# A hybrid attention and delta-rule step on one core: later products for transposed probabilities, and branch B's product with w_b during the second half's attention

## Chip, core and metric

The kernel runs on one core of a Trainium2 chip. The metric is the device time of one execution in microseconds, lower is better. Engines are named as in the profile: PE (TensorE, with PEld for its weight loads), DVE (VectorE), ACT (ScalarE), POOL (GpSimd) and SP (SyncE), which in this kernel issues every DMA.

## What is computed

One layer over 2048 prompt frames and 32 sampled frames of width 1024. The reference, cut to what the change touches:

```
qa, ka, va, za, qkv_b, zb, a_b, b_b, gate_a, gate_b = split_projection(x @ w_in)
oa = chunk_band_attention(qa, ka, va, rel_bias)      # 8 heads of 64, 9 chunks of 64 keys
ya = (oa * silu(za)) @ w_branch_a
ob, s_new = gated_delta_rule(...)                     # branch B, then a norm per head
yb = (ob * silu(zb)) @ w_branch_b
mix = sigmoid(gate_a) * ya + sigmoid(gate_b) * yb
y = layer_norm(ALPHA * x + mix @ w_out)
```

The newest 512 rows of k and v, and those of the sampled frames, are outputs too.

## The kernel before

The frames are worked off in two halves of 1024 (the second with the 32 sampled frames). For each half a stream of projection jobs (`all_jobs`, L2022; `multiply`) runs on TensorE: 128 columns of w_in times all frames of the half, split into a high and a low f16 part, so three products per 128 rows. Beside these jobs runs first branch B (`phase_b`), then attention (`phase_a`, L1492). After the second half's attention comes the merge (L2157): for each of 8 blocks of 256 frames the gated outputs of both branches are multiplied by w_a and w_b, weighted by the gates, added, multiplied by w_out and normalised.

**What sets the order.** The kernel is written as many small streams (Python generators) which a planner, the class `Flow`, runs while the program is built. It keeps a clock per engine, adds an estimated price for every instruction and DMA, and lets the stream go on that is earliest by these clocks. The result is a fixed order of instructions on each engine and of DMAs on SP's queue. On the chip every engine takes its instructions in that order and waits at each until its inputs are there. A price in the planner thus changes no work, only the order. `transfer` (L211) returns the time at which a DMA is thought to have landed; `turn` (L301) does so for a DMA transpose; `gate` and `places` are counted slots, `mark` an event.

**Attention.** Per pair of heads p, jobs v, k, q and z bring the operands. k and q are split into f16 high and low parts. `kst` holds for each head its high part in its own 64 partitions and the low part in the other 64; `qd` holds the high part of q in both; so one product over 128 rows gives high times high plus high times low. A second product, with the low part of q, completes the score (`score`, L1804). For it `ql` (`low_q`, L1523) is a tile of [128, 2, 1024] with zeros in the other head's partitions. The scores get their bias and maximum on VectorE, the exponential on ScalarE, and are split again into f16 parts `pu`. A DMA transpose turns `pu` into `pt`, with which TensorE makes the product with v into bank "c" (`product`). `store` (L1892) loads the gate `ga` (from za), transposes the normalised output in a "b" bank and writes the result to `g_dram[0]`. There are two "b" banks, three "a", two "pj" and one "c". Rows of k and v go out by `rows_out` (L1554): for each 128 rows a transpose into a "b" bank, a copy to one of two `ro` tiles and a DMA.

**Fetching.** `fetch` (L619) loads the weights of all jobs in order through two raw tiles, and after the last job w_a and w_b. `claim_w` (L771) gives them their room: w_a in a pool of its own, w_b in the room of the normalised input, which is free only after the last projection.

**Merge.** `load_g` (L2135) brings the branch outputs of a block and splits them, `sg_ahead` (L2253) the gates (three tiles per branch), and `merge` runs, for each of 8 column groups f and both branches, 12 products of 256 columns: four with the high and low part of the weights and the high part of g, then four with the low part of g. VectorE multiplies the sum by the gate (`evac`) and adds the branches (`fold`). For block 0 the order of (f, branch) starts with three groups of w_a (`order`, L2151).

Of the kernel before, what the change touches and what calls it, by code (L numbers as in the profile page):

```python
# [21 lines left out]
P = 128  # L22
# [37 lines left out]
MARGIN = 1.6  # L60
LEAD = 5.0
# [44 lines left out]
class Places(Gate):  # L106


    def __init__(self, flow, n):
        super().__init__(flow, n)  # L110
        self.numbers, self.first = deque(range(n)), False

    def ask(self, s):
        super().ask(s)
        if self.first and self.queue and self.queue[-1] is s:
            self.queue.rotate(1)
        self.first = False

    def take(self, first=False):
        self.first = first  # L120
        yield self
        return self.numbers.popleft()
# [97 lines left out]

def width(ap):
    n = 1
    for k in ap.shape[1:]:
        n *= k
    return n
# [52 lines left out]
def trunk(ctx: ExitStack, tc: tile.TileContext, x_p, x_s, cache_k, cache_v, st_conv, st_gdn,  # L278
# [22 lines left out]
    def turn(dst, src):  # L301

        nc.sync.dma_start_transpose(dst, src)
        n = 2 * P
        for k in dst.shape[1:]:
            n *= k
        return flow.transfer("SP", n * 1.5)
# [311 lines left out]
    def fetch(jobs):  # L619

        for job in jobs:
            yield raw_gate
            raw = wpool.tile([P, KD, P], F32, tag="wraw", bufs=NRAW, name="wraw")
            if job.cols < P:
                G.memset(raw[:], 0.0)
                yield
            for c0, part in job.src:
                for k0 in range(0, KD, 4):
                    t = dma(raw[:, k0:k0 + 4, c0:c0 + part.shape[2]], part[:, k0:k0 + 4, :])
            q_raw.put((job, raw, t))  # L630
            yield

        jobs_near.done()
        for br, w in enumerate((w_a, w_b)):
            yield from claim_w(br)
            for k in range(NP):
                yield raw_gate
                wr = wpool.tile([P, KD, P], F32, tag="wraw", bufs=NRAW, name="wr")
                wr = wr[:].rearrange("p k n -> p (k n)")
                t = dma(wr, w[k * P:(k + 1) * P, :])  # L640
                both = [None, raw_gate.give]
                for c in range(2):
                    flow.start(split_w(br, k, c, wr[:, c * 512:(c + 1) * 512], t, both[c]))
                yield
        for _ in range(NRAW):
            yield raw_gate
        front_w.done()

# [158 lines left out]
    def job_gate(half, br, f):  # L807
        def evac(bi, c0, n, gcol, ps):
            yield sig_slots
            t = wpool.tile([P, 512], F32, tag="sig", bufs=2, name="sig")  # L810
            S.activation(out=t[:, 0:n], in_=ps[:, 0:n], func=AF.Tanh, scale=w_half[:, wid:wid + 1])
            bank["pj"].give()
            yield
            yield dma(sig_dram[br][f][:, gcol:gcol + n], t[:, 0:n])
            sig_slots.give()

        wid = 32 + 8 * br + f
        return Job(half, wid, [(0, w_in[wid])], evac)

    rest = [[job_gate(half, br, f) for br in range(2) for f in range(KD)] for half in range(2)]  # L820


# [669 lines left out]
    def phase_a(half):  # L1492
# [8 lines left out]
        ro_slots, bias_slots, vs_slot, sample_slot = gate(2), [gate(2), gate(1)], gate(2), gate(1)  # L1501
# [21 lines left out]
        low_q = []  # L1523
        for i in range(2):
            t = ap.tile([P, 2, HALF], F16, name=f"ql{i}")
            for h in range(2):
                G.memset(t[HS[1 - h], h], 0.0)
            low_q.append(t)
# [25 lines left out]
        def rows_out(src, n, dst, p):  # L1554

            for t in range(0, n, P):
                m = min(P, n - t)
                yield bank["b"]
                ps = pt("b")
                PE.transpose(ps[:m, 0:P], src[:, t:t + m], ident[:])  # L1560
                yield ro_slots
                ro = ap.tile([P, P], F32, tag="ro", bufs=2, name="ro")
                S.copy(out=ro[:m], in_=ps[:m, 0:P])
                bank["b"].give()
                yield
                yield dma(dst[t:t + m, p * P:(p + 1) * P], ro[:m])
                ro_slots.give()

        def job_v(k):
# [9 lines left out]
            def rest():  # L1579
# [32 lines left out]
                if last:  # L1612
# [9 lines left out]
                    yield from rows_out(vf[:, KW:KW + DEC], DEC, nv_s, p)  # L1622
# [62 lines left out]
        def job_q(k):  # L1685
# [3 lines left out]
            def begin():  # L1689
# [11 lines left out]
                k.ql = ql = low_q[p % 2]  # L1701
# [102 lines left out]
        def score(h, k, t, w, place, before, turn_):  # L1804
# [8 lines left out]
            for i, (s0, sn) in enumerate(pieces):  # L1813
# [5 lines left out]
                PE.matmul(ps[:, 0:sn], ql[:, h, t * P:(t + 1) * P], kst[:, h, kc + s0:kc + s0 + sn],  # L1819
# [72 lines left out]
        def store(k, t, gt, w):  # L1892
# [7 lines left out]
            at = dma(ga[:], za_dram[k.p][:, gt * P:(gt + 1) * P])  # L1900
# [220 lines left out]
    g_slot, m_slot, x_slots = gate(1), gate(1), gate(3)  # L2121
    SGB = 3
    sg_slots = [gate(SGB), gate(SGB)]
    q_g, q_x, q_sg = [Queue(flow), Queue(flow)], [Queue(flow), Queue(flow)], Queue(flow)
# [9 lines left out]

    def load_g():  # L2135
        yield jobs_near
        for b in range(NB):
            c0 = b * FB
            n = FB if b < NB - 1 else FW
            yield g_slot  # L2140
            for br in range(2):
                ghi = gp.tile([P, NP, FW], F32R, tag=f"ghi{br}", bufs=1, name="ghi")
                glo = gp.tile([P, NP, FW], F32R, tag=f"glo{br}", bufs=1, name="glo")
                m = [[mark() for _ in range(NP)] for _ in range(2)]
                t = dma(glo[:, :, 0:n].bitcast(F32), g_dram[br][:, :, c0:c0 + n].rearrange("q p t -> p q t"))
                for p in range(NP):
                    flow.start(split_g(ghi, glo, p, m, n, t))
                q_g[br].put((ghi, glo, m))
                yield

    def order(b):  # L2151
        todo = [(f, br) for f in range(KD) for br in range(2)]
        if b == 0:
            todo.sort(key=lambda w: w[0] if w[0] >= SGB else w[1] - 2)
        return todo

    def merge():  # L2157
        yield jobs_done
        for b in range(NB):
            c0, n = b * FB, FB if b < NB - 1 else FW  # L2160
            gs = [None, None]
# [28 lines left out]

            all_parts, all_both = [[] for _ in range(KD)], [[0] for _ in range(KD)]
            for f, br in order(b):
                parts, both = all_parts[f], all_both[f]
                sg, t = yield from q_sg.get()
                parts.append(sg)
                yield bank["a"]
                ps = pt("a")
                if f == 0:
                    gs[br] = yield from q_g[br].get()
                gh, gl, ready = gs[br]  # L2200
                for k in range(NP):
                    yield w_ready[br, k, f // 4]
                    wh, wl = (w[f // 4][:, :, f % 4 * P:(f % 4 + 1) * P] for w in wres[br])
                    yield ready[0][k]
                    PE.matmul(ps[:, 0:n], wh[:, k], gh[:, k, 0:n], start=(k == 0), stop=False)
                    PE.matmul(ps[:, 0:n], wl[:, k], gh[:, k, 0:n], start=False, stop=False)
                    yield
                for k in range(NP):
                    yield ready[1][k]
                    PE.matmul(ps[:, 0:n], wh[:, k], gl[:, k, 0:n], start=False, stop=(k == NP - 1))  # L2210
                    yield

                def evac(f=f, sg=sg, ps=ps, t=t, parts=parts, both=both):
                    yield t
                    V.scalar_tensor_tensor(out=sg[:, 0:n], in0=sg[:, 0:n], scalar=1.0, in1=ps[:, 0:n],
                                           op0=ALU.add, op1=ALU.mult)
                    bank["a"].give()
                    yield
                    both[0] += 1
                    if both[0] == 2:  # L2220
                        yield from fold(f, parts)

                flow.start(evac())
            g_slot.give()

# [27 lines left out]
    def sg_ahead():  # L2253
        yield jobs_near
        for b in range(NB):
            n = FB if b < NB - 1 else FW
            for f, br in order(b):
                yield sg_slots[br]
                sg = gp.tile([P, FW], F32, tag=f"sg{br}", bufs=SGB, name="sg")
                t = dma(sg[:, 0:n], sig_dram[br][f][:, b * FB:b * FB + n])  # L2260
                q_sg.put((sg, t))
                if b == 0:
                    yield t - LEAD

# [80 lines left out]
    for half in range(2):  # L2345
# [5 lines left out]
        if half:  # L2351
# [3 lines left out]
            for gen in (load_g(), sg_ahead(), merge()):  # L2355
# [68 lines left out]
```

## Time and profile before

| | |
|---|---|
| time before, median of 3 runs | 2080.12 us (2076.62 to 2083.29) |
| the profiled execution: its time | 2078.09 us |
| its span, first to last instruction | 2076.3 us |
| mean granted TensorE clock | 0.973 |
| DMA transposes pt<-pu | 128 |
| loads of gates in the merge, sg<-sig | 128 |

A row of the windows gives the stretch, its length, the busy time of each engine with the number of instructions, the granted clock, the mean share of the 16 DMA engines and the data rate. A row of a tile gives the operation, the tile written and those read, the count, the minimum, median and maximum duration in ns, first and last start, and the shapes; 64*32 is 64 rows and 32 columns of the array. A row of the waits gives who waited for what, the total, how often, and the longest. A row in order of time gives start, duration, and in brackets the idle time before it and what ended it. Nearly every instruction bears the line of the helper that records it (L269; DMAs L292 and L303), so tiles tell them apart.

### The profile page before, as it was taken

The numbers are of one execution on the slowest core, as the hardware profiler recorded it, in microseconds if no ns is written. First come the engines' busy times: TensorE is split into PE (matmuls) and PEld (weight loads), VectorE is DVE, ScalarE is ACT, GpSimd is POOL, SyncE is SP. The second block draws the span as 40 slices with busy tenths as digits, with TensorE's granted clock in tenths as the row PEclk, the third lists the DMA queues.
The fourth block names the chain that finished last, engine by engine and source line by source line (L and its number), as shares of the span: only waits on it lengthen the run. The fifth ranks groups of instructions, "written<-read, shape, count | busy, mean of one in ns | idle before, by whom it ended". The sixth has DMA issues, their size and how long they took to land. (4 is left out here: it accounts for less than half of the span.)

```text
span 2076.3 us, 41078 instructions
## 1 busy us (share of the span) xinstructions
PE 1930.5 (93%) x14517; PEld 1353.4 (65%) x14517; DVE 1400.7 (67%) x4498; ACT 972.5 (47%) x2002; POOL 796.0 (38%) x1139
## 2 busy tenths in 40 slices
PE   8999999999989899999999999998888879999997
PEld 5455666665444446576776777665555568999996
DVE  7789889852556658589889884254545468665665
ACT  6655545444655667665445434354646552111110
POOL 6444334333334334443333423132323245543452
PEclk9999999999999999999999999999999989999999
DMA  4124332332587775223232333466776785433331
GB/s 138 65 87 112 87 85 75 102 90 98 140 201 158 163 171 135 69 81 87 74 84 67 94 98 90 117 142 146 158 167 148 186 217 193 132 102 122 103 124 46
DMA packets 380055, 246.85 MB, mean 119 GB/s; under 512 B 251202, under 2 KB 328366, under 8 KB 379848
## 3 DMA queue, kind: packets, MB, share of 16 engines
q1 hardware_dynamic: 379848, 244.22, 44.4%
q8 instruction: 114, 1.87, 0.4%
q14 instruction: 93, 0.76, 0.1%
HBM read 140.11 MB, written 54.72 MB: 94 GB/s over the span
## 5 line engine op out<-in xcount | busy, mean ns | idle before, releaser
L269 PE MATMUL pj<-hi,whi 128*128 128x512 f16 (+2 forms) x1992 | 651.3, 342 | 10.6 <-DVE zb L269 3.1
L269 PE MATMUL pj<-hi,wlo 128*128 128x512 f16 (+2 forms) x1952 | 643.6, 342 | 0.6 <-POOL wlo L269 0.5
L269 PEld LDWEIGHTS <-whi 128*128 128x128 f16 x3984 | 414.7, 106 | 226.0 <-issue 11.9
L269 PE MATMUL pj<-lo,whi 128*128 128x512 f16 (+2 forms) x1992 | 460.3, 343 | 0.0
L269 POOL TENSOR_TENSOR wlo<-wraw,whi 128x256 f16<-128x256 f32 x384 | 266.7, 718 | 497.4 <-ACT whi L269 369.5
L269 PEld LDWEIGHTS <-wlo 128*128 128x128 f16 x1952 | 207.1, 106 | 122.8 <-issue 16.6
L269 ACT CAST mh<-sg 128x256 fp32r<-128x256 f32 x64 | 25.8, 407 | 278.2 <-DVE sg L269 259.1
L269 ACT ACTIVATE wraw<-wraw,w_scale 128x1024 f32<-128x1024 f32 (+1 forms) x98 | 111.4, 1136 | 84.2 <-DVE w_scale L269 82.7
L269 ACT ACTIVATE sb<-sb,mx,unit 128x640 f32<-128x640 f32 (+4 forms) x128 | 108.5, 848 | 68.9 <-DVE mx L269 59.1
L269 PE MATMUL a<-ghi,whi 128*128 128x256 f32 (+1 forms) x512 | 134.4, 292 | 6.7 <-DVE sg L269 6.1
L269 POOL TENSOR_TENSOR pu<-sb,pu 128x640 f16<-128x640 f32 (+2 forms) x64 | 81.7, 1277 | 146.1 <-ACT pu L269 92.9
L269 ACT CAST whi<-wraw 128x512 f16<-128x512 f32 (+1 forms) x196 | 119.2, 611 | 33.3 <-PE pj L269 30.5
L269 PE MATMUL c<-vt,pt 128*128 128x64 f16 x1680 | 74.6, 198 | 64.5 <-DMA pt<-pu 61.4
L269 PE MATMUL a<-ghi,wlo 128*128 128x256 f32 (+1 forms) x512 | 132.0, 288 | 1.1 <-POOL wlo L269 1.0
L269 PEld LDWEIGHTS <-pt 128*128 128x128 f16 x1680 | 65.8, 101 | 98.8 <-DMA pt<-pu 87.1
L269 DVE TENSOR_TENSOR sys_u<-sys_u,sys_t 128x60 f32<-128x60 f32 (+24 forms) x527 | 124.6, 242 | 5.7
L269 DVE CUSTOM_DVE_ANT_0 sb<-a,bias 128x320 f32<-128x320 f32 (+5 forms) x136 | 66.5, 498 | 77.0 <-PE a L269 71.5
L269 DVE SCALAR_TENSOR_TENSOR acc<-raw,cwT,acc 128x512 f32<-128x512 f32 x144 | 112.8, 783 | 8.1 <-ACT acc L269 6.8
L269 DVE TENSOR_TENSOR sys_t<-sys_u,sys_p 128x60 f32<-128x60 f32 (+21 forms) x459 | 110.0, 243 | 5.5
L269 PEld LDWEIGHTS a<-ghi,whi 128*128 128x128 f32 x512 | 99.5, 194 | 8.3 <-DVE sg L269 6.7
L269 PEld LDWEIGHTS a<-ghi,wlo 128*128 128x128 f32 x512 | 98.9, 193 | 1.9 <-POOL wlo L269 1.2
L269 POOL TENSOR_TENSOR w_scale<-w_scale,mhalf 128x1 f32<-128x1 f32 x49 | 31.7, 648 | 168.1 <-DVE w_scale L269 120.0
(345 smaller groups left out, 4013.5 us busy)
## 6 DMA issues: line engine op xcount, KB each, us to landing
wraw<-in_w_in SPq DMA_DIRECT2D x192, 256.0 KB
sg<-sig SPq DMA_DIRECT2D x112, 128.0 KB
sig<-sig SPq DMA_DIRECT2D x44, 256.0 KB
sys_p<-sol_p SPq DMA_DIRECT2D x68, 128.0 KB
x<-in_x_p SPq DMA_DIRECT2D x16, 512.0 KB
xt<-in_x_p SPq DMA_DIRECT2D x16, 512.0 KB
out_y_p<-xt SPq DMA_DIRECT2D x16, 512.0 KB
glo<-g SPq DMA_DIRECT2D x14, 512.0 KB
```

Of the source, the lines that this page charges most:

```text
L269: r = f(*a, **k)
```

## The change

Four things are changed.

1. In the planner a transpose takes 0.8 us more of SP's queue and is thought to land SLACK = 2.5 us later; the load of `ga` gets the same 2.5 us.
2. `ql` is a tile of [128, 1024] without zeros. The second score product takes the 64 partitions of its head, of `ql` and of `kst`. One DMA per block of q fills it instead of two, and the zeros are no longer set.
3. `rows_out` transposes up to four groups of rows into one bank and writes them with one copy and one DMA (a remainder of less than 128 rows with another); there is one `ro` tile. The v rows of the sampled frames are written from `v_s`.
4. w_b is fetched before job z of pair 0 of the second half, into the pool that w_a had; w_a comes at the end, into the room of the normalised input. A new stream `early` starts when w_b is split. For block after block that the merge hasn't claimed it loads g of branch B, and for each f the gate; when the planner's TensorE has less than 0.2 us of work ahead, it makes the 12 products in a "b" bank, multiplies by the gate and writes the weighted result over the gate in DRAM. The merge leaves out branch B for such blocks and loads the finished values in the gate's place. Blocks 4 to 7 also wait for the second half's gates of branch B, whose jobs now come ahead of branch A's. `early` ends once w_out is ready.

```
-        return flow.transfer("SP", n * 1.5)
+        flow.busy["SP"] = max(flow.busy.get("SP", 0.0), flow.cur.clock + 0.2) + 0.8
+        return flow.transfer("SP", n * 1.5) + SLACK
...
+            if job.half == 1 and job.key == EARLY:
+                yield from load_w(1, w_b)
...
-        if br:
+        if br == 0:
             for g in h_free:
                 yield g
         else:
             yield wr_open
-        pool = hpool if br else wr_pool[0]
+        pool = wr_pool[0] if br else hpool
...
+    rest = [[job_gate(half, br, f) for br in ((0, 1) if half == 0 else (1, 0)) for f in range(KD)] for half in range(2)]
...
-                    t = dma(ql[HS[h], h, cs], lo[HS[h], 0:m])
+                t = dma(ql[:, cs], lo[:, 0:m])
...
-                PE.matmul(ps[:, 0:sn], ql[:, h, t * P:(t + 1) * P], kst[:, h, kc + s0:kc + s0 + sn],
+                PE.matmul(ps[:, 0:sn], ql[HS[h], t * P:(t + 1) * P], kst[HS[h], h, kc + s0:kc + s0 + sn],
                           start=False, stop=True)
...
-            at = dma(ga[:], za_dram[k.p][:, gt * P:(gt + 1) * P])
+            at = dma(ga[:], za_dram[k.p][:, gt * P:(gt + 1) * P]) + SLACK
```

The new rows_out and the new stream:

```
+            yield bank["b"]
+            ps = pt("b")
             for t in range(0, n, P):
                 m = min(P, n - t)
+                PE.transpose(ps[:m, t:t + P], src[:, t:t + m], ident[:])
+            yield ro_slots
+            ro = ap.tile([P, 512], F32, tag="ro", bufs=1, name="ro")
+            if full:
+                S.copy(out=ro[:, 0:full * P], in_=ps[:, 0:full * P])
...
+                at = dma(dst[0:full * P, cs].rearrange("(t q) d -> q t d", q=P),
+                         ro[:, 0:full * P].rearrange("q (t d) -> q t d", d=P))
...
+    def early():
+        for k in range(NP):
+            for c in range(2):
+                yield w_ready[1, k, c]
+        for b in range(NB):
+            c0, n = b * FB, FB if b < NB - 1 else FW
+            if b in claimed_b or w_ready["o", KD - 1, 1].at is not None:
+                return
+            claimed_b[b] = "early"
+            yield g_early
+            g = get_g(1, b)
+            for f in range(KD):
+                if b == NB // 2:
+                    yield gate_done[1, 1, f]
+                yield sge_slots
+                sg = gp.tile([P, FW], F32, tag="sge", bufs=2, name="sge")
+                t = dma(sg[:, 0:n], sig_dram[1][f][:, c0:c0 + n])
+                while w_ready["o", KD - 1, 1].at is None and flow.busy["PE"] > flow.cur.clock + 0.2:
+                    yield flow.busy["PE"]
+                yield bank["b"]
+                ps = pt("b")
+                yield from branch(1, f, n, ps, g, t - MARGIN)
...
+                    V.scalar_tensor_tensor(out=sg[:, 0:n], in0=sg[:, 0:n], scalar=1.0, in1=ps[:, 0:n],
+                                           op0=ALU.add, op1=ALU.mult)
+                    bank["b"].give()
+                    yield
+                    yield dma(sig_dram[1][f][:, c0:c0 + n], sg[:, 0:n])
+                    sge_slots.give()
...
+            g_early.give()
```

More of the change, by code (lines that the diff above doesn't have):

```diff
@@ L110, in __init__, with take @@
         super().__init__(flow, n)
[L111 to L120, printed above, removed]
+        self.numbers = deque(range(n))
+    def take(self):
         yield self
@@ L633, in fetch @@
         jobs_near.done()
[L634 to L644, printed above, removed]
+        yield from load_w(0, w_a)
         for _ in range(NRAW):
@@ L2151, in order, with claim_block @@
[L2151 to L2155, printed above, removed]
+            gs = [get_g(0, b)]
+            if not claim_block(b):
+                yield g_early
+                gs.append(get_g(1, b))
+            q_g.put(gs)
+            yield
+    def claim_block(b):
+        if b not in claimed_b:
+            claimed_b[b] = "merge"
+        return claimed_b[b] == "early"
@@ L2189, in fold @@
                 m_ready[1][f].done()
[L2191 to L2195, printed above, removed]
+            g = None
+            for f in range(KD):
+                parts = []
+                for br in range(2):
+                    parts.append((yield from q_sg.get()))
                 yield bank["a"]
@@ L2208, in merge @@
[L2208 to L2213, printed above, removed]
-                    yield t
[L2215 to L2221, printed above, removed]
```

153 lines of the change are left out of this document (100 added, 53 removed).

## Prediction

> **What bounds the kernel now.** I read the page first, then five stretches of the span, then TensorE's waits in the two attention stretches, then single moments of them in order of time.
>
> ```profile
> span 2076.3 us, 41078 instructions
> PE 1930.5 (93%) x14517; PEld 1353.4 (65%) x14517; DVE 1400.7 (67%) x4498; ACT 972.5 (47%) x2002; POOL 796.0 (38%) x1139
> ```
>
> TensorE (PE) is busy for 93% of the span, so the kernel is bound by TensorE's work and by the holes in it. The windows say where the holes are; the columns are busy time per engine, the granted TensorE clock, the DMA share and GB/s.
>
> ```profile
> core 0: us, PE busy (x) PEld busy (x) DVE busy (x) ACT busy (x) POOL busy (x), PEclk, DMA share, GB/s
> 500.00:820.00 320.00, 286.98 (x2089) 158.00 (x2087) 189.19 (x687) 197.88 (x389) 120.18 (x153) 0.97 0.68 162
> 820.00:1290.00 470.00, 454.91 (x3840) 333.96 (x3840) 382.09 (x1318) 233.94 (x501) 178.51 (x317) 0.98 0.29 80
> 1290.00:1662.00 372.00, 323.63 (x2712) 210.72 (x2711) 172.01 (x598) 196.54 (x407) 100.32 (x111) 0.95 0.66 153
> 1662.00:1700.00 38.00, 29.74 (x298) 24.71 (x297) 25.49 (x85) 19.05 (x39) 11.35 (x9) 0.82 0.75 176
> 1700.00:2076.00 376.00, 359.33 (x2247) 323.81 (x2245) 240.66 (x424) 55.68 (x143) 171.94 (x208) 0.99 0.39 125
> ```
>
> The first row is the first half's attention: 320 - 287.0 = 33.0 us without TensorE work. The third and fourth are the second half's attention, first beside the projections, then alone: 48.4 + 8.3 = 56.7 us. The last is the merge; it is nearly full (16.7 us idle), and DMA is little used there. The stage to look at is therefore attention. Who ends TensorE's waits there (total us, times, longest), first half and then second:
>
> ```profile
> PE c L269 <- DMA pt<-pu: 25.5, 19, 3.3
> ```
>
> ```profile
> PE c L269 <- DMA pt<-pu: 35.9, 23, 3.8
> PE b L269 <- DVE ga L269: 6.2, 6, 2.3
> PE b L269 <- ACT za L269: 2.8, 1, 2.8
> ```
>
> Two thirds of the idle time, 61.4 us, is the product of the probabilities with v waiting for their transposes (pt<-pu, by DMA). TensorE takes its instructions in an order fixed at build time, and the build thought the transposes would land earlier than they do. Such a wait costs more than itself:
>
> ```profile
> 1439.68 0.28 PE L269 MATMUL pj<-hi,whi 128*128 128x272 f16 x1
> 1439.80 0.28 PE L269 MATMUL pj<-hi,wlo 128*128 128x272 f16 x1
> 1442.53 0.61 PE L269 MATMUL c<-vt,pt 128*128 128x64 f16 x15 [2.46 <-DMA pt<-pu]
> ...
> 1443.70 0.43 PE L269 MATMUL pj<-hi,whi 128*128 128x272 f16 x1
> 1443.93 0.43 PE L269 MATMUL pj<-hi,wlo 128*128 128x272 f16 x1
> ```
>
> Before the wait of 2.46 us the same product started every 0.12 us, about a microsecond after it every 0.23 us: the clock is at half. The windows give the price: TensorE's busy time times the missing clock is 287.0 x 0.03 = 8.6, 323.6 x 0.05 = 16.2 and 29.7 x 0.18 = 5.4 us, 30 us in all. So the waits on transposes stand for up to 61.4 + 30 = 91 us. [...]
>
> **Room for the transposes.** The planner (which only decides the order) now charges each transpose 0.8 us more on SyncE's queue and lets it land another 2.5 us later, so 3.3 us of other work is put ahead of each product with v. That is as long as the longest wait of the first half (3.3 us) and nearly that of the second (3.8), so on an unchanged pipeline almost all 91 us would go. What is late next is SyncE, which issues every DMA, transposes among them:
>
> ```profile
> 1450.02 0.44 SPq L292 DMA_DIRECT2D g<-ga  x1
> ...
> 1498.47 1.89 SPq L292 DMA_DIRECT2D kst<-part  x3
> ```
>
> ```profile
> L303 SPq DMA_TRANSPOSE pt<-pu x128: 1167/1356/2562, 550.7 to 1691.0; - x128
> ```
>
> Between these first and last rows lie 51 issues that take 41.8 of 50 us, a transpose alone 1.36 us. With SyncE at 84%, part of the lateness is a queue and not a wrong estimate; an order with later products does not shorten that queue. I take 60% of 91: **-55 us**, ends 0 and -91. The same 2.5 us is given to the load of za (ga<-za), which stands behind the 6.2 us of "DVE ga" above; I count it with the holes below.
>
> **Low part of q without its zeros.** Half of each zero-padded tile goes, so the second score product contracts over 64 rows instead of 128. It has the same columns, but another shape. What a change of shape costs is seen where the sampled frames' 64-row product stands between projections, and at a transpose over 32 rows and the full width:
>
> ```profile
> 1647.48 0.28 PE L269 MATMUL pj<-hi,whi 128*128 128x272 f16 x1
> 1647.60 0.28 PE L269 MATMUL pj<-hi,wlo 128*128 128x272 f16 x1
> 1647.81 0.24 PE L269 MATMUL a<-ks,qs 64*32 64x32 f32 x2
> 1647.98 0.29 PE L269 MATMUL pj<-hi,whi 128*128 128x272 f16 x1
> ```
>
> ```profile
> 1649.47 0.28 PE L269 MATMUL pj<-hi,wlo 128*128 128x272 f16 x1
> 1649.59 0.28 PE L269 MATMUL pj<-hi,whi 128*128 128x272 f16 x1
> 1649.80 0.46 PE L269 MATMUL b<-ident,sb 32*128 32x32 f32 x5
> ```
>
> ```profile
> L269 PE MATMUL a<-kst,ql x224: 217/299/490, 544.5 to 1686.4; 128*128 128x320 f16 x96, 128*128 128x384 f16 x7, 128*128 128x512 f16 x5, 128*128 128x128 f16 x4
> ```
>
> From 272 columns to the next start are 0.12 us, but 0.21 us when the next is a 64-row product or the 32-row one: 0.09 us to enter. Leaving is between nothing and the same 0.09; two 32-column products in 0.17 us (1647.81 to 1647.98) leave room for most of it, so I take 0.16 for both ways. 224 products x 0.16 = **+36 us**, ends 20 and 42 (224 x 0.09 and x 0.19). It lies on TensorE in the attention stretches, where TensorE is the bound; only inside a wait that remains would it be hidden. [...] The edit also saves 20 DMA issues (of 40) and 8 fills on POOL; neither is what ends last.
>
> **Rows written out.** Four transposes share a bank, one copy and one DMA; the v rows of the 32 sampled frames go out from an existing tile. Four transposes of TensorE, 28 copies or so and 16 issues less, one buffer instead of two. Counted at nothing: ScalarE is busy 196.5 of 372 us there, which covers it.
>
> **w_b beside attention.** w_b is fetched ahead of the fourth projection of the second attention instead of at the end, and the early stream works off branch B for blocks of 256 frames: 8 units each of load gate, 12 products, one VectorE evacuation, write back.
>
> ```profile
> 1742.04 0.28 PE L269 MATMUL a<-ghi,whi 128*128 128x256 f32 x1
> ...
> 1743.46 0.28 PE L269 MATMUL a<-ghi,whi 128*128 128x256 f32 x1
> ```
>
> ```profile
> L292 SPq DMA_DIRECT2D sg<-sig x128: 319/423/1559, 1595.3 to 2036.8; - x128
> L292 SPq DMA_DIRECT2D sig<-sig x84: 319/327/632, 30.5 to 1666.2; - x84
> ```
>
> A unit is 1.42 us of TensorE, a block 11.4, all eight 91 us. Moving them is no gain by itself: what the merge loses, attention gets. The gain is the holes they fill. Besides transposes, the second half has 56.7 - 35.9 = 20.8 us of holes; most are a fraction of a microsecond to 2.8 us in a fixed order, where a unit only helps if it was put just there. I take **-8 us**, ends 0 and -21. The moved steps bring their queues: 16 further issues a block, 8 x (0.42 + 0.33) = 6 us of SyncE, 48 us for all eight, against about 12 saved in this half (28 issues, also at 0.42); 16.8 MB more through the DMA engines, by the merge's row (125 GB/s at a share of 0.39, so 320 GB/s at 1) 52 us of all sixteen, over some 430 us a share of about 0.12 on top of 0.66. New waits: the evacuation waits on VectorE for its gate, with the score reductions queued behind it, and keeps one of two "b" banks that the output transposes need; the write back waits on SyncE with pt<-pu behind it. VectorE has room (172 of 372 us busy), SyncE hardly. I take **+5 us**, ends 0 and +25. When the projections end, w_a now comes last as w_b did; the cover for that are early units still to do.
>
> The merge loses 11.4 us a block and stays bound by TensorE: VectorE is busy 240.7 of 376 us there, and its evacuations of branch B leave with the products.
>
> **Sum**: -55 + 36 - 8 + 5 = -22 us. The profiled execution took 2078.1 us (its span and 1.8 around it), the median of the runs shown is 2080.1; against that, 2058 us.
>
> **Rivals.** *SyncE paces attention (slower, 0.24).* With 16 more issues per block the transposes slip by as much as the order gives them, TensorE waits as before, and the change of shape is paid in full: 2080 + 36 - 8 = 2108 us. It decides once less than 33 us of the 91 come back. For it: 41.8 of 50 us; transposes that took up to 2.56 us to issue. Against it: the attention stretch gets 91 us of TensorE work and so lasts longer, which leaves SyncE near its present share.
>
> *Nothing to be seen (0.12).* The clock does not recover, since shorter waits remain between longer work: 60% of 61 = 37 us come back, -37 + 36 - 8 + 5 = -4, 2076 us. The rows after the 2.46 us wait speak against it. [...]
>
> *Early hardly runs (faster, 0.15).* A unit starts only when the planner's TensorE has less than 0.2 us ahead of it. If the plan is always full, two or three blocks are done early: -55 + 36 - 2 + 1, 2060 us.
>
> *No price for the shape (faster, 0.10).* If 64 rows at full width change nothing, 2058 - 36 = 2022 us; no row excludes it.
>
> **How the numbers follow.** The forecast itself has 0.39, with 2020 to 2074 as its own range. About 0.3% (6 us) is what a measurement of this kernel can tell from no change: faster 0.39 + 0.15 + 0.10 = 0.64, same 0.12, slower 0.24. Below 2015 I leave 0.08 (almost all waits gone and no price for the shape), above 2096 about 0.12, the worse half of the slower rival.
>
> **What would show it.** Right: PE c's wait on pt<-pu under 30 us over both halves; clock above 0.97 in the second attention; a<-kst,ql in shape 64*128, with starts about 0.09 us late before or after it; branch B's products in bank b from about 1370 us on, at most a few left in the merge; a merge some 80 us shorter, and an attention longer by less than that. Wrong: waits on pt<-pu of 50 us or more while SyncE has no gaps, or ql with no delay before or after it, or waits of TensorE for w_a of over 10 us after the last projection.

## The result and the profile after

| | before | after |
|---|---|---|
| time, median | 2078.72 us (2076.62 to 2083.29, 4 runs) | 2098.34 us (2092.11 to 2100.53, 4 runs) |
| the profiled execution | 2078.09 us, span 2076.3 | 2092.11 us, span 2090.3 |

After to before 1.0083, 95% interval 1.0067 to 1.0099: the change makes the kernel slower, by about 19.6 us. The forecast was 2058 us, faster, with a range from 2015 to 2096. The profiled execution of the changed kernel is the fastest of its four, so its trace holds 14.0 us of these 19.6.

The page of the changed kernel, and the windows that the prediction showed of before, with one more for the last 14 us:

```profile
span 2090.3 us, 41148 instructions
PE 1973.3 (94%) x14513; PEld 1348.3 (64%) x14513; DVE 1405.1 (67%) x4498; ACT 970.6 (46%) x1982; POOL 786.8 (38%) x1131
```

```profile
core 0: us, PE busy (x) PEld busy (x) DVE busy (x) ACT busy (x) POOL busy (x), PEclk, DMA share, GB/s
500.00:820.00 320.00, 304.73 (x2118) 155.91 (x2117) 197.14 (x694) 200.30 (x394) 119.91 (x153) 0.97 0.67 162
...
1290.00:1662.00 372.00, 355.51 (x2837) 232.97 (x2835) 177.25 (x598) 187.60 (x378) 96.71 (x111) 0.98 0.72 172
1662.00:1700.00 38.00, 38.00 (x388) 26.42 (x387) 21.90 (x84) 19.99 (x43) 7.41 (x7) 1.00 0.66 150
1700.00:2076.00 376.00, 338.51 (x1981) 292.69 (x1980) 230.18 (x417) 60.62 (x148) 175.27 (x207) 0.95 0.44 138
2076.00:2090.30 14.30, 5.78 (x26) 4.45 (x24) 5.61 (x8) 0.00 (x0) 1.46 (x1) 0.82 0.18 73
```

Attention did what was wanted: TensorE is busy for 355.5 of 372 us (323.6 before) at a clock of 0.98 (0.95), and 38.0 of 38. The merge went the other way: 338.5 of 376 us busy (359.3), at 0.95 (0.99). TensorE's waits, first half's attention, then the second's (1280 to 1730 us), then the merge (from 1730 us):

```profile
PE c L266 <- DMA pt<-pu: 0.3, 1, 0.3
...
PE b L266 <- ACT ghi L266: 5.6, 2, 3.5
PE b L266 <- ACT ro L266: 3.0, 3, 1.7
...
PE c L266 <- DMA pt<-pu: 0.5, 1, 0.5
...
PE pj L266 <- ACT mh L266: 20.7, 11, 3.5
PE a L266 <- DVE sg L266: 5.1, 7, 2.3
```

The waits on pt<-pu fell from 61.4 us to 0.8. In their place stand 20.7 us in which the output products of the merge wait for mh, the merged rows that ScalarE has just converted. In the kernel before, the merge's waits were 2.7 us in all:

```profile
PE pj L269 <- DVE ms L269: 1.2, 1, 1.2
PE a L269 <- DVE sg L269: 0.8, 1, 0.8
PE pj L269 <- POOL ms L269: 0.7, 1, 0.7
```

The early stream's rows, and the first and last output products of the merge:

```profile
L266 DVE SCALAR_TENSOR_TENSOR sge<-sge,b x48: 406/422/423, 1350.3 to 1783.2; 128x256 f32<-128x256 f32 x48
L266 PE MATMUL b<-woh,mh x128: 387/390/564, 1761.9 to 2079.3; 128*128 128x512 f32 x128
```

```profile
L269 PE MATMUL b<-woh,mh x128: 388/389/389, 1725.7 to 2065.5; 128*128 128x512 f32 x128
```

48 units are done early, that is blocks 0 to 5; 45 of them lie ahead of the first output product into bank b (upper row after, lower row before). In the kernel before, the 8 units of block 0 had to be done by then too. So 37 units, 37 x 1.42 = 52.5 us of TensorE, were moved ahead of that product, and it comes only 36.2 us later: 16.3 us of them were recovered. From the first to the last such product pass 317.4 us instead of 339.8, 22.4 less, although 52.5 us of work are gone from there. The missing 30.1 us are the loss. 36.2 - 22.4 = 13.8 us, the 14.0 of the span.

The merge waits like this (blocks 0 to 5, in which TensorE has only branch A to do, are called light below); TensorE, SyncE, VectorE and ScalarE in order of time:

```profile
1874.44 0.39 PE L266 MATMUL pj<-wol,mh 128*128 128x512 f32 x1
1877.94 0.79 PE L266 MATMUL pj<-woh,mh 128*128 128x512 f32 x1 [3.12 <-ACT mh L266]
1878.54 0.63 PE L266 MATMUL pj<-wol,mh 128*128 128x512 f32 x1
...
1873.07 1.74 SPq L289 DMA_DIRECT2D sg<-sig  x4
...
1876.33 0.42 DVE L266 SCALAR_TENSOR_TENSOR sg<-sg,a 128x256 f32<-128x256 f32 x1 [2.96 <-DMA sg<-sig]
1877.03 0.43 DVE L266 TENSOR_TENSOR sg<-sg 128x256 f32<-128x256 f32 x1 [0.27 <-DMA sg<-sig]
...
1877.49 0.40 ACT L266 CAST mh<-sg 128x256 fp32r<-128x256 f32 x1 [3.67 <-DVE sg L266]
```

Read from the bottom: ScalarE waits for VectorE, VectorE for a gate that SyncE had issued at 1873.07 or later, and TensorE for both. After the wait TensorE's first products start every 0.60 us instead of every 0.24. Part of this is the clock, which is recorded at half from 1877.0 to 1883.8 us.

### The profile page after: what moved, and what is told of

It is laid out like the page before. It is cut to its first block, busy times and chain, and to the rows that moved or that the text cites. A ratio compares the mean times of both kernels' runs of the same rounds, so it can differ in the third digit from the quotient of the medians.

```text
span 2090.3 us, 41148 instructions
## 1 busy us (share of the span) xinstructions
PE 1973.3 (94%) x14513; PEld 1348.3 (64%) x14513; DVE 1405.1 (67%) x4498; ACT 970.6 (46%) x1982; POOL 786.8 (38%) x1131
## 4 chain that ended last, share of the span: by engine, by line
PE 62%; DVE 16%; DMA 7%; issue 5%; ACT 4%; POOL 4%; SPq 2%; POOLq 0%; DVEq 0%; ACTq 0%
PE pj L266 37%; PE b L266 12%; PE a L266 6%; PE x L266 3%; DVE acc L266 2%; PE c L266 2%; DVE sys_t L266 2%; SPq L289 2%; DVE sys_u L266 2%; DMA sg<-sig 2%; PE o L266 2%; POOL wlo L266 1%; POOL xt L266 1%; DVE sg L266 1%; DVE kd_bd L266 1%
## 5 line engine op out<-in xcount | busy, mean ns | idle before, releaser
L266 PE MATMUL pj<-hi,whi 128*128 128x512 f16 (+2 forms) x1992 | 650.1, 341 | 15.8 <-ACT vf L266 3.3
L266 PEld LDWEIGHTS <-whi 128*128 128x128 f16 x3984 | 408.3, 105 | 235.8 <-issue 13.3
L266 PE MATMUL pj<-lo,whi 128*128 128x512 f16 (+2 forms) x1992 | 468.2, 341 | 0.0
L266 ACT COPY v_t<-o 128x64 f32<-128x64 f32 x132 | 27.7, 210 | 144.1 <-PE o L266 107.7
L266 PE MATMUL a<-ghi,whi 128*128 128x256 f32 (+1 forms) x320 | 82.9, 289 | 6.4 <-DVE sg L266 5.1
L266 ACT ACTIVATE sig<-pj,w_half 128x512 f32<-128x512 f32 (+2 forms) x84 | 49.3, 587 | 78.2 <-PE pj L266 72.7
L266 PE MATMUL a<-ghi,wlo 128*128 128x256 f32 (+1 forms) x320 | 82.1, 286 | 3.2 <-DVE wlo L266 1.6
L266 ACT CAST pu<-sb 128x640 f16<-128x640 f32 (+4 forms) x128 | 81.8, 649 | 4.4 <-DMA pt<-pu 4.2
```

What stands on the lines that cost most here:

```text
L266: r = f(*a, **k)
```

## Experiments

The theory after this comparison: the early stream is what costs, through the light blocks of the merge; the forecast's gain from the room for transposes is mostly eaten by the shape of ql. The rivals: the shape alone, and the room worth nothing. All times below are medians; the kernel before, measured again beside each, took 2079 to 2081 us.

**One part alone: the shape of ql.**

```
-                    t = dma(ql[HS[h], h, cs], lo[HS[h], 0:m])
+                t = dma(ql[:, cs], lo[:, 0:m])
...
-                PE.matmul(ps[:, 0:sn], ql[:, h, t * P:(t + 1) * P], kst[:, h, kc + s0:kc + s0 + sn],
+                PE.matmul(ps[:, 0:sn], ql[HS[h], t * P:(t + 1) * P], kst[HS[h], h, kc + s0:kc + s0 + sn],
                           start=False, stop=True)
```

> The kernel before with one part of the change alone: the low part of q without its zeros (second score product over 64 rows). Theory A, the change of shape costs TensorE about 0.2 us per product wherever it stands: 224 of them, so 30 to 42 us slower, 2110 to 2120 us, with TensorE busy some 40 us longer. Theory B, the cost falls into the waits on transposes that are there anyway: under 10 us slower, 2079 to 2088 us.

2090.88 us, ratio 1.0056 (1.0038 to 1.0073): between the two theories, nearer to B. TensorE is busy for 1969.4 us instead of 1930.5:

```profile
PE 1969.4 (94%) x14517; PEld 1344.4 (64%) x14517; DVE 1399.3 (67%) x4498; ACT 972.4 (46%) x2002; POOL 790.6 (38%) x1131
```

The price on TensorE is there in full, 38.9 us, but only 11.7 us of it reach the time: two thirds lie in waits that were there anyway (the second half's waits on pt<-pu fell from 35.9 to 25.3 us). What one product pays is seen in the changed kernel, between products of 512 columns:

```profile
608.14 0.38 PE L266 MATMUL a<-kst,qd 128*128 128x512 f16 x1
608.36 0.38 PE L266 MATMUL pj<-hi,wlo 128*128 128x512 f16 x1
608.67 0.39 PE L266 MATMUL a<-kst,ql 64*128 64x512 f16 x1
608.99 0.61 PE L266 MATMUL pj<-lo,whi 128*128 128x512 f16 x2
```

0.22 us from start to start, then 0.31 into the 64-row product and 0.32 out of it: 0.09 and 0.10.

**One part alone: the planner's prices.**

```
+SLACK = 2.5
...
-        return flow.transfer("SP", n * 1.5)
+        flow.busy["SP"] = max(flow.busy.get("SP", 0.0), flow.cur.clock + 0.2) + 0.8
+        return flow.transfer("SP", n * 1.5) + SLACK
...
-            at = dma(ga[:], za_dram[k.p][:, gt * P:(gt + 1) * P])
+            at = dma(ga[:], za_dram[k.p][:, gt * P:(gt + 1) * P]) + SLACK
```

> The kernel before with the planner's new prices for transposes and for the load of ga alone; no instruction differs, only the order. Theory A, the waits on pt<-pu were a wrong order and nothing else: they fall from 61 us to under 5, the clock comes back, 40 to 60 us faster, 2020 to 2040 us. Theory B, the wait only moves to other operations of attention (bank, copy, output), or SyncE holds the pace: less than 20 us faster, 2060 to 2079 us.

2073.41 us, ratio 0.9976 (0.9955 to 0.9997): theory B. The waits on pt<-pu fall to 9.5 + 10.3 = 19.8 us, and 5.7 us of time come of it. TensorE's waits in the second half's attention, and the two attention stretches:

```profile
PE b L270 <- ACT ro L270: 17.9, 13, 3.7
PE c L270 <- DMA pt<-pu: 10.3, 7, 2.3
...
PE pj L270 <- ACT kr L270: 5.1, 4, 1.8
PE pj L270 <- DVE zs L270: 4.8, 2, 2.8
```

```profile
500.00:830.00 330.00, 302.99 (x2225) 169.97 (x2224) 202.08 (x704) 206.29 (x406) 127.98 (x165) 0.97 0.69 163
1280.00:1730.00 450.00, 388.70 (x3185) 266.62 (x3184) 225.96 (x734) 232.79 (x476) 133.23 (x142) 0.92 0.68 165
```

For comparison the second stretch of the kernel before:

```profile
1280.00:1730.00 450.00, 387.44 (x3228) 263.82 (x3226) 225.20 (x734) 234.55 (x481) 136.97 (x147) 0.94 0.68 166
```

450 - 388.7 = 61.3 us of idle time, 62.6 before, and a lower clock: the wait only changed its name. Banks that ScalarE's copies of rows have not freed, k rows and z come late next.

**The same prices taken out of the changed kernel.** (The edit is the one above, undone; SLACK is then unused.)

> The changed kernel with the old prices in the planner, so that the products with v are ordered as early as before; everything else of the change stays. The prices alone, in the kernel before, were worth 5.7 us, although the waits on pt<-pu fell by 41.6. Theory A (they are worth more here, because the units of the early stream are what is put ahead of the products with v): waits on pt<-pu are 40 us or more again and the time is 2112 to 2130. Theory B (they are worth the same here as there): 2100 to 2108.

2124.14 us, ratio 1.0220 (1.0192 to 1.0249): theory A by the time. In the company of the rest the prices are worth 25.8 us, not 5.7; waits on pt<-pu are 14.3 + 17.5 = 31.8 us, under the 40 that A named. That the early units are what makes the prices worth more here is not shown by itself.

**Without the early stream.**

```
-            for gen in (early(), load_g(), sg_ahead(), merge()):
+            for gen in (load_g(), sg_ahead(), merge()):
```

> The changed kernel without the early stream: w_b is still fetched early, but all products with w_b are made in the merge. Theory A, early gives nothing net, since attention had few holes left and the merge loses its cover (holes of 20 us and half clock there): 5 to 30 us faster than the changed kernel, 2070 to 2093 us. Theory B, early does fill holes: 15 to 30 us slower than the changed kernel, 2113 to 2128 us.

2079.03 us, ratio 1.0001 (0.9992 to 1.0011): theory A. The other three parts cancel, and the early stream costs 19.3 us. TensorE's waits after 1730 us are 2.7 us in all, as in the kernel before. The output products into bank b:

```profile
L266 PE MATMUL b<-woh,mh x128: 388/389/389, 1724.6 to 2063.5; 128*128 128x512 f32 x128
```

Against this kernel the early stream alone brings the first one 37.3 us later for 52.5 us of moved work, so 15.2 us are recovered; from first to last pass 21.5 us less, so 31.0 us are lost. The difference, 15.8 us, is that of the spans (2090.3 and 2074.5 us).

**Light and heavy blocks in turn.**

```
-        for b in range(NB):
+        for b in range(1, NB, 2):
...
-                if b == NB // 2:
+                if b >= NB // 2:
```

> The changed kernel, but the early stream takes only the odd blocks 1, 3, 5, 7, so that in the merge a block with one product alternates with a block with two. Theory A, the merge with one product per block is held up by VectorE's folds and normalisation, and by work of early that runs after attention's end: its waits on mh fall to under 6 us, 10 to 20 us faster than the changed kernel, 2078 to 2088 us. Theory B, the holes of the merge come from late gates or from DMA and stay: within 5 us of 2098, or slower as less is done early.

2098.58 us, ratio 1.0095 (1.0069 to 1.0122). Here 32 units are done early instead of 48. TensorE's waits on mh are 11.9 us, for four light blocks instead of six, so about 3 us per light block as in the changed kernel, and not under the 6 us of theory A. A light block between two heavy ones waits about as long, which speaks against what I took for VectorE's backlog from one block to the next.

**VectorE's norm left out, with and without the early stream.**

```
-        V.scalar_tensor_tensor(out=xt[:rows], in0=xt[:rows], scalar=m2[:rows, 0:1], in1=rowv["lng"][:rows],
-                               op0=ALU.subtract, op1=ALU.mult)
...
-        V.scalar_tensor_tensor(out=xt[:rows], in0=xt[:rows], scalar=m2[:rows, 1:2], in1=rowv["lnb"][:rows],
-                               op0=ALU.mult, op1=ALU.add)
```

> This kernel is the changed one with VectorE's last two operations of the layer norm left out (the product with lng and the last scale and shift), so its output is not normalised; they are two operations of VectorE on each group of output rows in the merge, and nothing of TensorE. Theory A (in the merge, a block whose branch B is already done has half the products of TensorE but all of VectorE's folds and normalisation; VectorE paces it, the fold is late and the output products wait for mh): TensorE's waits on mh in the merge fall from 20.7 to under 6 us, and the kernel takes 2065 to 2080 us instead of 2098. Theory B (the output products wait for the gates that come by DMA or for something else than VectorE's queue): waits on mh stay over 12 us and the time is within 8 us of the changed kernel, 2090 or more.

> The control to the run before it: the changed kernel without the early stream, with the same two operations of the layer norm left out (output not normalised). Without the early stream the merge waits only 2.6 us in all, so under theory A the two operations are hidden and this kernel takes the same as the one without the early stream, 2079 us, within 5 us; the kernel with the early stream and without the operations is then 5 to 15 us faster than this one, that is, the early stream pays once VectorE does not pace the merge. Theory B: the early stream still costs 10 us or more against this one.

The output is then not normalised; TensorE's products come in the same order as in the changed kernel or in the one without the early stream. 2094.92 us (ratio 1.0075, 1.0049 to 1.0100) and 2074.21 us (0.9969, 0.9956 to 0.9982). With less work on VectorE the waits on mh are 24.6 us, not fewer: the early stream still costs 20.7 us. My theory that VectorE paces the light blocks falls. VectorE itself stood waiting for gates here (1820 to 1985 us):

```profile
DVE sg L266 <- DMA sg<-sig: 15.8, 13, 2.9
```

**The gates loaded further ahead.** That left the gates' buffers. A gate's tile is free only when the fold and the low part of mh are done with it, and there are three per branch. SyncE's waits between 1820 and 1985 us (blocks 2 to 5) of the changed kernel, with TensorE's and VectorE's there:

```profile
PE pj L266 <- ACT mh L266: 12.9, 6, 3.5
...
DVE sg L266 <- DMA sg<-sig: 13.8, 12, 3.1
...
SPq L289 <- DVE xt L266: 49.4, 4, 12.7
SPq L289 <- POOL ml L266: 24.6, 14, 3.7
SPq L289 <- DVE ml L266: 24.0, 8, 6.7
```

SyncE stands before the next load until POOL or VectorE has made ml and so freed the tile (the last two rows). Its longest waits, 49.4 us, are another thing: there it stands before a store of output rows until VectorE has finished them (xt). In the experiment every second gate of these blocks goes into branch B's g tiles, which then lie idle:

```
-                    yield sg_slots[br]
-                    sg = gp.tile([P, FW], F32, tag=f"sg{br}", bufs=SGB, name="sg")
+                    own = spare is None or f % 2 == 0
+                    slots = sg_slots[br] if own else sgx_slots[br]
+                    yield slots
...
+                        sg = spare[br][:, f // 2].bitcast(F32)
```

> The changed kernel, in which the gates of the merge's blocks 2 to 5 (branch B done early) are loaded up to 7 per branch ahead instead of 3: every second one goes into the two tiles of branch B's g, which lie idle in these blocks. TensorE's order of work is the same. In the changed kernel, and just so without the last two operations of the norm, TensorE waits once in each of these blocks for mh, 2.9 to 3.5 us (4.1 to 4.7 there), and each time VectorE was itself waiting for a gate (sg<-sig) whose load SyncE had issued late. Theory A (three buffers pace a block that has only half of TensorE's products: a gate's buffer comes free after the fold and the low part of mh, and only then is the next load issued): these four waits vanish, waits on mh and sg in the merge fall from 25.8 to about 12 us, the clock there rises from 0.95 to 0.97 or more, and the kernel takes 2074 to 2086 us. Theory B (the loads are late because the transfers or SyncE are): the waits stay over 20 us and the time is 2092 to 2102.

2075.88 us, ratio 0.9984 (0.9966 to 1.0002): theory A, 22.5 us faster than the changed kernel, with the same order of TensorE's work. In the same stretch:

```profile
PE pj L266 <- ACT mh L266: 1.1, 4, 0.3
...
DVE sg L266 <- PE a L266: 5.0, 9, 0.9
```

VectorE now waits for TensorE (PE a) and no longer for gates. The output products run to 2064.4 us, though they begin at 1767.1:

```profile
L266 PE MATMUL b<-woh,mh x128: 388/389/628, 1767.1 to 2064.4; 128*128 128x512 f32 x128
```

297.3 us instead of 317.4. TensorE between 1820 and 1985 us, first in the changed kernel, then with the gates ahead:

```profile
1820.00:1985.00 165.00, 150.98 (x828) 129.15 (x827) 98.14 (x172) 20.01 (x53) 81.53 (x99) 0.95 0.38 122
1820.00:1985.00 165.00, 163.95 (x992) 145.18 (x991) 111.79 (x199) 22.21 (x59) 93.21 (x115) 1.00 0.41 134
```

So three buffers were the cause of the loss in blocks 2 to 5. SyncE's waits before the stores of output rows are even longer here, 75.9 us, and TensorE waits for mh only 1.1 us; so they are not what cost the time.

**Rows written out.** Two runs. The old form of rows_out in the kernel without the early stream:

```
-            ro = ap.tile([P, 512], F32, tag="ro", bufs=1, name="ro")
+                ro = ap.tile([P, P], F32, tag="ro", bufs=2, name="ro")
```

> The changed kernel without the early stream (2079.0 us), in which the rows written out have their old form: a transpose, a copy and a DMA for each 128 rows, two buffers. So this is the kernel before with the prices for the transposes and the new low part of q. By their own single runs those two parts give -5.7 and +11.8 us, together 2085. Theory A (fewer copies of ScalarE free the banks sooner): the waits on ro, 3.6 us without the old form, rise to 10 us or more and the time is 2083 to 2092. Theory B (rows written out are worth nothing, as forecast): 2076 to 2081.

2095.66 us, ratio 1.0072 (1.0050 to 1.0094), 16.6 us slower than with the new form. But the waits on ro are 6.7 us, under A's 10, and the idle time is not larger. Second half's attention, first with the old rows, then with the new ones:

```profile
1280.00:1730.00 450.00, 407.24 (x3116) 249.28 (x3115) 211.61 (x704) 224.99 (x460) 120.44 (x134) 0.88 0.65 150
```

```profile
1280.00:1730.00 450.00, 403.68 (x3174) 253.94 (x3173) 230.97 (x732) 231.31 (x458) 128.50 (x137) 0.92 0.69 165
```

The difference is the clock: 407.2 x 0.12 = 49 us against 403.7 x 0.08 = 32. And the other way round, the kernel before with the prices and a new rows_out in groups of 256 rows (the change has up to 512), with one buffer instead of two:

```
+            for t0 in range(0, n, 256):
...
+                ro = ap.tile([P, 256], F32, tag="ro", bufs=1, name="ro")
```

> The kernel before with two parts of the change alone: the planner's prices for the transposes, and the rows written out by fewer copies (here two transposes to one copy and one DMA, the v rows of the sampled frames from the existing tile). The old zero-padded low part of q and no early stream. The prices alone gave 2073.4 us, with 61 us of TensorE still idle in the second half's attention, 17.9 of it waiting for a bank that ScalarE's copy to ro had not yet freed. Theory A (those copies are what came late once the transposes had room): TensorE's waits on ro fall under 6 us and the time to 2056 to 2067 us. Theory B (the copies only carry the name, and what is late next takes their place): waits on ro fall but the idle time of that stretch stays over 50 us, and the time is 2069 to 2076.

2086.45 us, ratio 1.0037 (1.0022 to 1.0053), 13 us slower than with the prices alone; the waits on ro rose from 17.9 to 25.1 us.

Both theories miss. Fewer copies, with one buffer, don't free the banks sooner by themselves; the form of the rows changes which order comes out, and that is worth over 10 us in either direction. Why, and what the number of buffers has to do with it, stays open.

**The old ql beside the early stream.** To make room for it in the kernel with the gates ahead, the gates have two tiles per branch of their own and the early stream one. The first kernel has this alone, the second the old ql with it:

```
-    SGB = 3
+    SGB = 2
```

> The control for the next run: the kernel with the gates loaded ahead, with less room: two buffers per branch for the gates of the merge instead of three, and one instead of two for the early stream. Expected somewhat slower than 2076 us, by 0 to 15, as the blocks without an early branch B and the early units have less ahead.

> The same kernel with the old zero-padded low part of q, for which the smaller buffers make room; so this pair gives the price of the 64-row shape beside the early stream. In the kernel before, the new shape cost 39 us of TensorE's busy time but 11.8 us of time, since two thirds fell into waits that were there. Theory A (here the waits are mostly filled, so the price is paid in full): this kernel is 25 to 42 us faster than the one before it in this list, which would make it the fastest, 2040 to 2060 us. Theory B (it is hidden as before, or what comes late next takes its place): 0 to 15 us faster.

2109.40 us (ratio 1.0144, 1.0121 to 1.0168) and 2113.74 us (1.0166, 1.0140 to 1.0193). One tile less per branch, and one less for the early stream, cost 33.5 us, more than the 15 at most that were expected. It fits the theory of the buffers but is no clean test of it, since with one tile the early stream does only 32 units instead of 48. The old ql is no faster here, against both theories: TensorE is busy 26.6 us less with it (1945.8 instead of 1972.4), and all of that is waiting again.

**The early stream on later blocks.** Again in the kernel with the gates ahead:

```
-        for b in range(NB):
+        for b in range(2, NB):
```

> The kernel with the gates loaded ahead (2075.9 us), with the early stream taking blocks 2 and on instead of 0 and on, so that the merge begins with two blocks that have both branches to do, and branch B's last early units no longer stand ahead of the merge's first output rows. In the kernel with the gates ahead 18.2 us of TensorE's time after 1730 us are idle, 16 of them before 1845 us, in blocks 0 and 1. Theory A (those waits come from block 0 and 1 needing units of branch B that were only just done, and from short blocks right at the start): waits after 1730 us fall under 8 us and the kernel takes 2058 to 2070 us. Theory B (they come from the start of the merge itself: output weights, g, first gates): idle time of the start stays at 12 us or more, and the time is within 6 us of 2076.

2086.17 us, ratio 1.0039 (1.0022 to 1.0057): theory B by the idle time, though the time is 10 us above B's 2076. TensorE waits 8.1 us up to 1735 us for a bank that VectorE has to empty, with the preparation of the output weights (wol) ahead in its queue, and 7.7 us for g between 1790 and 1830 us; the start of the merge has waits of its own, which this order makes larger.

No version beats both kernels by more than a measurement tells: the prices alone (0.9976) and the gates ahead (0.9984) lie at 0.2%.

## Why the prediction was wrong

Two steps failed: the merge does not stay bound by TensorE when branch B is moved out of it, and the waits on transposes were not worth what they add up to.

**The early stream (-8 + 5 = -3 forecast, +19.3 measured).** This step turned a gain into a loss: "The merge loses 11.4 us a block and stays bound by TensorE: VectorE is busy 240.7 of 376 us there, and its evacuations of branch B leave with the products." No engine became the bound. What did not shrink with the products is the ring of each gate: load, multiply, fold, low part, release, load. Each light block still needs 16 loads through 3 + 3 tiles, and the branch products that cover them fell from 22.8 us to 11.4. With seven tiles per branch the early stream is worth 2075.9 - 2079.0 = -3.1 us. That this is the forecast's figure is luck, and it is too small to be told from nothing: there, too, the first output product into bank b comes 42.5 us later than without the early stream and the stretch of them is 41.6 us shorter, so of 52.5 us of moved work 10.0 are recovered and 10.9 lost, for the most part in blocks 0 and 1 (15 us idle from 1730 to 1845 us). The +5 for SyncE was not what decided in attention: waits on pt<-pu are 0.8 us.

**Room for the transposes (-55 forecast; -5.7 alone, -25.8 with the rest).** The mechanism held: the waits on pt<-pu went. The size failed with "on an unchanged pipeline almost all 91 us would go", of which 60% was taken. A fixed order has other results that are nearly as late; ro, kr, zs and za took over at once (with the prices alone 61.3 us of the second stretch are idle, 62.6 before), and the clock, counted with 30 us, did not recover in the second half (0.94 to 0.92). I named only SyncE as late next. (Its 41.8 of 50 us were added up from rows that hold the gaps between issues too; the 51 issues alone take 40.3 us.)

**The shape of ql (+36 forecast; 38.9 us of TensorE, 11.7 of time alone).** The price per product was right (0.16 forecast, 0.19 measured between two 512-column products), as was the total on TensorE. What failed is that it was counted in full, because attention is where "TensorE is the bound". The condition beside it, "only inside a wait that remains would it be hidden", was right: so much waiting remained that two thirds were hidden alone and all in the last pair. Put on top of the prices it cost 2095.7 - 2073.4 = 22.3 us.

**Rows written out (nothing forecast; -16.6 measured, and +13.0 for groups of 256 rows in another company).** ScalarE's 196.5 of 372 us said nothing on it; the effect is on order and clock.

Taken one after the other (prices, ql, rows, early stream), the parts give -5.7 + 22.3 - 16.6 + 19.3 = +19.3 us. That this is the measured result follows from how they were taken and proves nothing; each difference is uncertain by about 5 us, and in another order the terms would be others. Against the forecast's -55 + 36 + 0 - 3 = -22, the room misses by 49 us and the early stream by 22, both to the slow side, ql by 14 and the rows by 17 to the fast side.

**The chances.** Slower had 0.24, with SyncE's queue as its mechanism. That rival did not come true; the time came out on its side for a reason that was not on the list. The range ended 2.3 us below the median. The signs for attention came true: waits on pt<-pu 0.8 us, clock 0.98, the 64-row starts 0.09 us late, branch B in bank b early. Two failed: a merge some 80 us shorter (22.4 us between the first and the last output product), and at most a few units left in the merge (16 of 64).

## What to carry to other kernels

When work is moved out of a stage, ask what in that stage is not moved: buffers that are loaded, used and released once per step can pace it once the work that covered them is halved, with no engine being the bound (here three tiles per branch instead of seven cost 22.5 us). In a fixed order a wait that ends last gives way to the next late result, so a sum of waits of one name is seldom the estimate (41.6 us less of them gave 5.7 us with the prices alone); try the part alone. And a price on the bounding engine is paid in time only where that engine does not wait anyway (the shape alone cost 38.9 us of TensorE and 11.7 us of time).

## What the runs showed of the hardware

The clock's records change in steps of 3.41 us (half clock from 1443.6 to 1447.0 us in the kernel before; from 624.3 to 637.9, four steps, in the changed one). In the kernel before, between 500 and 1730 us, no such window with more than 1.9 us of idle time was followed by full clock, and the 18 of the attention stretches that went from full to half held 1.56 to 3.20 us of it: waits shorter than the window were enough there. Of the four between 830 and 1280 us one held 2.65 us and three 0.5 us or less, which idle time in that window does not explain.

The half clock lasted longer in some stretches with 64-row products. The kernel before, around its wait of 2.46 us, and the one with the new ql alone, around a wait of 1.82 us:

```profile
1440.20:1443.60 3.40, 1.07 (x21) 1.03 (x22) 1.26 (x6) 0.43 (x2) 0.00 (x0) 1.00 0.93 185
1443.60:1447.00 3.40, 3.40 (x29) 2.46 (x28) 0.48 (x3) 0.00 (x0) 0.00 (x0) 0.50 0.37 82
1447.00:1453.80 6.80, 6.80 (x42) 3.99 (x41) 3.66 (x17) 4.65 (x9) 1.30 (x2) 1.00 0.76 221
```

```profile
1400.70:1407.50 6.80, 4.98 (x47) 3.44 (x46) 4.91 (x17) 5.83 (x13) 2.16 (x2) 1.00 0.63 140
1407.50:1421.20 13.70, 13.70 (x83) 7.35 (x81) 6.25 (x27) 4.61 (x11) 0.64 (x1) 0.50 0.67 120
1421.20:1428.00 6.80, 6.80 (x61) 3.73 (x60) 3.14 (x11) 6.30 (x15) 2.07 (x4) 1.00 0.42 92
```

In the first the clock is back after 3.4 us of work without a gap, in the second only after 13.7 us of work without a gap. Counted over the attention stretches of the eleven kernels with the new ql, 25 of 104 half-clock windows of 3.4 us without a gap were followed by another; of the four with the old one, 1 of 44 (the kernel before: none of 14). But 10 of the 25 stand in one kernel, that with the old rows, and the changed kernel has none among its 5. The longer half clock may be a second price of the change of shape, beside the 0.09 and 0.10 us; whether the shape is the cause was not tried by itself.
